# Expert loop of a hybrid decoder: one branch a step, chunk operations ahead of the next split, one transposition for crowded experts

## The chip, the cores and the metric

The kernel runs on one core of one Trainium2 chip, as one program. The metric is the device time of an execution in microseconds (us). Before the change three runs took 1495.41, 1495.72 and 1496.64 us; the median is 1495.72 us. The profiled execution took 1494.7 us, of which 1492.9 us lie between its first and last instruction (the span).

## What is computed

A trunk of two layers on 256 tokens of width 1024. Each layer has a mixer (a gated linear attention group and a state space group) and a feed-forward part. In the first layer that is a dense SwiGLU, in the second a mixture of eight SwiGLU experts, of which each token uses two:

```python
def moe_swiglu(h, router_w, w_gate, w_up, w_down):
    t = h.reshape(bsz * seq, d)
    logits = (t @ router_w).astype(jnp.float32)
    top_v, top_i = lax.top_k(logits, TOP_K)
    top_p = jax.nn.softmax(top_v, axis=-1)
    gates = jnp.sum(jax.nn.one_hot(top_i, N_EXPERTS) * top_p[..., None], axis=1)
    for e in range(N_EXPERTS):
        out = out + gates[:, e:e + 1] * swiglu(t, w_gate[e], w_up[e], w_down[e])
# swiglu(t, g, u, d) = (silu(t @ g) * (t @ u)) @ d;  g and u are 1024 x 3584, d is 3584 x 1024, all float32
```

A token without an expert has the gate zero there, so the kernel computes for each expert only the tokens that chose it.

## The kernel before

Every weight comes from memory as float32, in items of 1 MB (128 partitions by 2048 numbers), each once. It is split in two numbers of a reduced float32 type ("fp32r"): ScalarE writes the high part (L182), VectorE subtracts it from the original and writes the low part (L183). Products are then three matmuls: high by high, low by high, high by low. `pump` (L154) issues loads on SyncE's queue as soon as a raw buffer is free, that is, once its split is done. `fill` splits the next item into free slots; `w_done` frees the slots of an item whose matmuls have been issued, and calls `fill`. In the expert stage ten slots hold five split items, so what `w_done` issues after a step is the split of the item five steps later. The order in which operations are issued in the program is the order in which each engine's queue runs them.

The experts run one after the other, `run_experts` writing out the whole order. The hidden width 3584 is cut in seven chunks of 512. A chunk has six steps, one item each: gate (G) first and second half, up (U) first and second half, and down (D) first and second half of the chunk before. The very last chunk's down steps are called L. Up to 128 tokens of an expert are gathered into X, tokens on the matmul's stationary side, so that gate and up rows come out with tokens on partitions. After U's second half the chunk operations follow, each put at a step by `put` into `due`:

- `copy` (L1245): ScalarE copies the finished gate or up rows out of PSUM, at once
- `gate`: TensorE transposes the gate rows in four blocks (L1253 or L1255), ScalarE takes SiLU (L1273)
- `hidden`, two steps later: TensorE transposes the up rows, VectorE multiplies (L1283)
- `parted`, three steps later: ScalarE (L1293) and VectorE (L1294) split the product for the down steps

If an expert has at most 64 tokens ("narrow"), a token takes two rows, one for the high and one for the low part: two matmuls do instead of three (L1203, L1209), and instead of a transposition a matmul with the matrix `fold` adds the two rows (L1253). Else it is "wide": three matmuls (L1205, L1206, L1209) and plain transpositions (L1255). Which one holds is known only on the chip, so `modal` issues both forms in a branch (`tc.If`, L1193). The matmuls of a step have a branch on TensorE alone, each of `gate`, `hidden` and `parted` one on TensorE, ScalarE and VectorE. After a step's matmuls come, in this order: `done()` with the next split, then the chunk operations due, then `at`, which at given steps combines the expert before into the sum (L1624), and prepares the next one: its token maps, their transposition (`slots_T`, L1598), and its gathered and split tokens (`split_slots`, through `split_cols`, L498).

Experts are ordered on the chip so that full and sparse ones alternate; in this run places 1, 3 and 5 (from 0) are wide.

Of the kernel before, what the change touches and what calls it, by code (L numbers as in the profile page):

```python
# [17 lines left out]
P = 128  # L18
# [10 lines left out]
MOE_SLOTS = ("ra", "rb")  # L29
MOE_TURNED = 4  # L30
NH = 4
HALF = P // 2

HANDOFF_SPLITS = ((1, 1, 0, 1), (1, 1, 0, 1))
# [16 lines left out]
def trunk(ctx: ExitStack, tc: tile.TileContext, a: dict, out: bass.AP):  # L51
# [11 lines left out]
    def nm(s):  # L63
        uid[0] += 1
        return f"{s}_{uid[0]}"
# [4 lines left out]
    def ps_t():  # L70
        return psum.tile([P, 512], F, name=nm("pt"), tag="t", bufs=1)
# [261 lines left out]
    pe.transpose(pt[:, :DK], c_rows, ident[:DK, :DK])  # L333
    act.activation(s_col, pt[:, :DK], AF.Silu)

    tri = const.tile([P, P], F, name="tri")
    dve.tensor_scalar(tri, jp, 0.0, None, op0=OP.is_ge)
    btri = const.tile([P, P], F, name="btri")
    dve.tensor_scalar(btri, jp, 0.0, 1.0 / 16.0, op0=OP.is_ge, op1=OP.mult)
    dve.memset(btri[0:64, 64:128], 0.0)  # L340
    bmask = btri.bitcast(I32)
# [149 lines left out]
    def split_tmp(src, scale):  # L491
        return main.tile([P, len(scale), src.shape[-1]], F, name=nm("sct"), tag="rt", bufs=2)

    def split_cols(dst_h, dst_l, src, scale, shift=None):

        tmp = split_tmp(src, scale)
        scaled(act, tmp, src, scale, shift)
        dve.tensor_copy(dst_h, tmp)  # L498
        dve.tensor_tensor(dst_l, tmp, dst_h.bitcast(F), op=OP.subtract)

    def split_pair(a0, a1, mid=None):
# [733 lines left out]

    def run_experts(mo, experts, operand, fold, at):

        gs, us, sil, th, ys, ops = {}, {}, {}, {}, {}, {}
        due, ps = {}, {}
        order = list(moe_order(experts))  # L1240
        where = {t: n for n, t in enumerate(order)}

        def copied(tag, p):
            out = mo.tile([P, FC], F, name=nm(tag), tag=tag)
            act.activation(out, p, AF.Copy)  # L1245
            return out

        def folded(src, nar, p):

            for k in range(4):  # L1250
                ks = slice(k * P, (k + 1) * P)
                if nar:
                    pe.matmul(p[:, ks], src[:, ks], fold, start=True, stop=True)  # L1253
                else:
                    pe.transpose(p[:, ks], src[:, ks], ident)  # L1255
            return p

        def blocks(t, nar):
            return t.rearrange("p (k t) -> p k t", k=4)[:, :, :HALF if nar else P]

        def put(n, f, *args):
            due.setdefault(n, []).append((f, args))

        def copy(kind, key):
            (gs if kind == "G" else us)[key] = copied("gs" if kind == "G" else "us", ps.pop((kind,) + key))

        def gate(key):
            src, p = gs.pop(key), ps_t()
            s = sil[key] = mo.tile([P, FC], F, name=nm("fsg"), tag="fsg")

            def body(nar):
                folded(src, nar, p)
                act.activation(blocks(s, nar), blocks(p, nar), AF.Silu)  # L1273

            modal(ops[key[0]][2], body)

        def hidden(key):
            src, p, s = us.pop(key), ps_mm(), sil[key]

            def body(nar):  # L1280
                folded(src, nar, p)
                sv = blocks(s, nar)
                dve.tensor_tensor(sv, blocks(p, nar), sv, op=OP.mult)  # L1283

            modal(ops[key[0]][2], body)

        def parted(key):
            t = th[key] = mo.tile([P, 4, P, 2], R, name=nm("fth"), tag="fth", bufs=2)
            s = sil.pop(key)

            def body(nar):
                sv, tv = blocks(s, nar), t[:, :, :HALF if nar else P]
                act.activation(tv[:, :, :, 0], sv, AF.Copy)  # L1293
                dve.tensor_tensor(tv[:, :, :, 1], sv, tv[:, :, :, 0].bitcast(F), op=OP.subtract)  # L1294

            modal(ops[key[0]][2], body)

        for n, (kind, e, c, i) in enumerate(order):
            key = (e, c)
            if (kind, c, i) == ("G", 0, 0):  # L1300
                ops[e] = operand(e)
            X, narrow, _ = ops[e]
            if kind in "GU" and not i:
                ps[(kind,) + key] = ps_mm()
            if (kind, c, i) == ("D", 0, 0):
                ys[e] = ps_pair()
            parts, done = whole()
            dsts = []
            for k0, m, wh, wl in parts:
                for k in range(m):  # L1310
                    if kind in "GU":
                        kk = 4 * i + k0 + k
                        dsts.append((ps[(kind,) + key], X[:, kk], wh[:, k], wl[:, k], kk == 0, kk == 7))
                    elif kind == "L":
                        dsts.append((ys[e][i], th[key][:, k0 + k], wh[:, k], wl[:, k], False, k0 + k == 3))
                    else:
                        kk = 2 * i + k0 + k
                        for hf in range(2):
                            hs = slice(hf * 512, (hf + 1) * 512)
                            dsts.append((ys[e][hf], th[key][:, kk], wh[:, k, hs], wl[:, k, hs], c == 0 and kk == 0,  # L1320
                                         c == NFC - 1 and kk == 3))
            modal(narrow, lambda nar: mm_slots(dsts, nar))
            done()
            if kind in "GU" and i:
                put(n, copy, kind, key)
            if (kind, i) == ("U", 1):
                lag = 1 if key == (experts[-1], NFC - 1) else 2
                put(n, gate, key)
                put(n + lag, hidden, key)
                put(n + lag + 1, parted, key)  # L1330
            for f, args in due.pop(n, ()):
                f(*args)
            if kind in "GU":
                at(e, c, "GU".index(kind) * 2 + i, ys)
            elif kind == "D":
                e1, c1 = (e, c + 1) if c + 1 < NFC else (experts[experts.index(e) + 1], 0)
                at(e1, c1, 4 + i, ys)
            else:
                at(e, NFC, i, ys)
        assert not due  # L1340
        return ys[experts[-1]]
# [41 lines left out]
    def moe(mo, ys, row, mT):  # L1383
# [9 lines left out]
        mr = mo.tile([P, 2, 8], F, name="mr")  # L1393
        mb = mo.tile([P, 2, 8], BF, name="mb")
        gates = mo.tile([P, 2, 8], F, name="gates")
        pos = mo.tile([P, 2, 8], F, name="pos")
        cnt = mo.tile([P, 8], F, name="cnt")
        cmx = mo.tile([P, 1], F, name="cmx")
        cmi = mo.tile([P, 1], I32, name="cmi")
        shc = mods[:, l, 3]  # L1400
# [3 lines left out]
        pool.memset(onesb, 1.0)  # L1404
        iota_s = mo.tile([P, P], F, name="iota_s")
        pool.iota(iota_s, pattern=[[1, P]], base=0, channel_multiplier=0, allow_small_or_imprecise_dtypes=True)
        iota_h = mo.tile([P, P], F, name="iota_h")
        pool.iota(iota_h, pattern=[[1, HALF], [0, 2]], base=0, channel_multiplier=0, allow_small_or_imprecise_dtypes=True)
        fold = mo.tile([P, P], F, name="fold")
        pool.iota(fold, pattern=[[-2, P]], base=0, channel_multiplier=1, allow_small_or_imprecise_dtypes=True)  # L1410
        pm2 = mo.tile([P, 2, P], F, name="pm2")
        dve.tensor_scalar(pm2[:, 0], fold, 0.0, None, op0=OP.is_ge)
# [81 lines left out]
        pe.matmul(pp[:, 16:24], onesb, mb[:, 1], start=False, stop=True)  # L1494
        for t, r in enumerate((r0, r1)):
            dve.tensor_scalar(mr[:, t], mb[:, t], r, None, op0=OP.mult)
        dve.tensor_copy(pos, pp[:, 0:16].rearrange("p (t e) -> p t e", t=2))
        dve.tensor_scalar(few, pp[:, 16:24], float(HALF), None, op0=OP.is_le)

        def second_weights():  # L1500
# [2 lines left out]
            pool.tensor_tensor(pr[:, :, 1], euler, pr[:, :, 0], op=OP.pow)  # L1503

        def make_gates():
            dve.tensor_copy(cnt, pp[:, 16:24])
            dve.tensor_reduce(cmx, cnt, axis=AX.X, op=OP.max)
            dve.tensor_scalar(cmi, cmx, float(-P), 0.0, op0=OP.add, op1=OP.max)
            dve.tensor_scalar(pr[:, :, 0:1], pr[:, :, 1:2], 1.0, None, op0=OP.add)
            dve.reciprocal(pr[:, :, 0:1], pr[:, :, 0:1])  # L1510
            dve.tensor_tensor(pr[:, :, 1:2], pr[:, :, 1:2], pr[:, :, 0:1], op=OP.mult)
            for t in range(2):
                dve.tensor_scalar(gates[:, t], oh[:, t, 0], pr[:, t, 0:1], None, op0=OP.mult)
                dve.scalar_tensor_tensor(gates[:, t], oh[:, t, 1], pr[:, t, 1:2], gates[:, t], op0=OP.mult, op1=OP.add)
# [75 lines left out]
        def slots_T(e, pm, ps=ps_t, narrow=None):  # L1590
            pT = pTs[:, e % 2]
            p = ps()
            def body(nar):
                for t in range(2):
                    pe.transpose(p[:, t * P:(t + 1) * P], (pm2 if nar else pm)[:, t], ident)

            modal(narrow, body)
            dve.tensor_scalar(pT, p[:, :256].rearrange("p (t s) -> p t s", t=2), 0.0, None, op0=OP.is_gt)  # L1598
            return pT

        def y_split(y, hf, row=None):
# [73 lines left out]
        def split_slots(e, hf):  # L1675
            dst, (src, scale, shift) = gathered(e, hf), gather(m["pm"], hf, free)

            def body(nar):
                w = HALF if nar else P
                split_cols(*[d[:, :, :w] for d in dst], src[:, :, :w], scale, shift)  # L1680

            modal(narrow[e][1], body)

# [213 lines left out]
```

## Time and profile before

| | |
|---|---|
| median of three runs | 1495.72 us |
| profiled execution | 1494.7 us |
| its span | 1492.9 us |
| TensorE matmuls busy | 1400.3 us (94%) |
| VectorE busy | 1286.0 us (86%) |
| ScalarE busy | 1052.4 us (70%) |
| read from memory | 480.12 MB, 322 GB/s over the span |

Busy times of matmuls overlap, because the next starts before the one before has ended; where TensorE works without a gap the distance of starts tells its pace. The page cuts the span into 40 slices of 37.3 us; the experts take the time from about the sixteenth slice on. Idle time is listed with what ended it.

### The profile page before, as it was taken

To read this page: it belongs to the slowest core of one execution; us is meant where nothing else is said; L and a number is where in the kernel's file an instruction comes from. 1 tells how busy PE (TensorE), PEld (TensorE's weight loads), DVE (VectorE), ACT (ScalarE), POOL (GpSimd) and SP (SyncE) were. 2 spreads that over 40 slices of the span, in tenths; PEclk is the share of its full clock that TensorE was granted. 3 is DMA by queue.
4 is the path that set the end of the run, shared out by engine and by line. 5 is a ranking of instruction groups with operands and counts; after the bars stand their busy time and mean duration, and the time that the engine had idled before them with its cause. 6 is when DMAs were issued, how large, how long until landed. Compare 5 with 4: busy or idle time off the path is not lost.

```text
span 1492.9 us, 22114 instructions
## 1 busy us (share of the span) xinstructions
PE 1400.3 (94%) x7578; PEld 1200.1 (80%) x7578; DVE 1286.0 (86%) x1186; ACT 1052.4 (70%) x1255; POOL 46.6 (3%) x74
## 2 busy tenths in 40 slices
PE   5998899999999998999999999999999999998986
PEld 4886699999879776788888778888788888877764
DVE  7888877777766659999889999988999988999996
ACT  3484654544557557798778888778898777888885
POOL 2011000000010011000000000000000000000001
PEclk9999999999999998999999999999999999999998
DMA  9974678888844456999999999999999999999994
GB/s 345 313 253 164 231 277 311 314 312 320 298 170 142 150 174 221 342 394 393 393 341 370 393 393 395 393 364 366 390 394 392 394 375 357 387 393 395 393 392 153
DMA packets 204618, 483.29 MB, mean 324 GB/s; under 512 B 13119, under 2 KB 15405, under 8 KB 204462
## 3 DMA queue, kind: packets, MB, share of 16 engines
q1 hardware_dynamic: 203890, 480.05, 87.7%
q8 instruction: 99, 1.62, 0.5%
q10 hardware_dynamic: 428, 0.63, 0.1%
q0 software_dynamic: 144, 0.52, 0.1%
q14 instruction: 57, 0.47, 0.1%
HBM read 480.12 MB, written 1.05 MB: 322 GB/s over the span
## 4 chain that ended last, share of the span: by engine, by line
PE 69%; DVE 13%; DMA 6%; issue 6%; ACT 5%; POOL 1%; DVEq 0%; ACTq 0%; SPq 0%; POOLq 0%
PE mm L1209 9%; PE y L1209 5%; PE mm L1205 5%; PE mm L1206 5%; DVE ws L183 4%; PE mm L1203 4%; PE mm L430 4%; PE mm L429 4%; PE mm L431 4%; PE y L429 3%; PE y L431 3%; PE y L430 3%; PE y L1203 3%; PE y L1205 3%; PE y L1206 3%
## 5 line engine op out<-in xcount | busy, mean ns | idle before, releaser
L174 ACT ACTIVATE ws<-raw 128x1024 fp32r<-128x1024 f32 x136 | 143.9, 1061 | 139.6 <-PE mm L431 61.4
L183 DVE TENSOR_TENSOR ws<-raw,ws 128x2048 fp32r<-128x2048 f32 x97 | 222.1, 2291 | 15.9 <-ACT ws L182 15.8
L175 DVE TENSOR_TENSOR ws<-raw,ws 128x1024 fp32r<-128x1024 f32 x136 | 164.5, 1222 | 57.5 <-ACT ws L174 57.1
L182 ACT ACTIVATE ws<-raw 128x2048 fp32r<-128x2048 f32 x97 | 185.7, 1916 | 24.6 <-PE mm L1206 12.0
L1205 PE MATMUL mm<-ws,hTl 128*128 128x512 f32 x336 | 134.9, 402 | 0.0
L1206 PE MATMUL mm<-ws,hTl 128*128 128x512 f32 x336 | 132.6, 395 | 0.0
L1203 PE MATMUL mm<-ws,hTh 128*128 128x512 f32 x448 | 125.9, 403 | 4.9 <-ACT gs L1245 2.7
L1209 PE MATMUL y<-ws,fth 128*128 128x512 f32 x448 | 124.4, 400 | 0.0
L1209 PE MATMUL mm<-ws,hTh 128*128 128x512 f32 x448 | 122.4, 395 | 0.0
L1209 PE MATMUL mm<-ws,hTl 128*128 128x512 f32 x448 | 122.1, 394 | 0.0
L183 DVE TENSOR_TENSOR ws<-xm,ws 128x2048 fp32r<-128x2048 f32 x46 | 105.4, 2290 | 14.0 <-ACT ws L182 14.0
L367 DVE SCALAR_TENSOR_TENSOR ada<-raw,s_col,ada 128x1024 f32<-128x1024 f32 (+1 forms) x98 | 112.2, 1145 | 2.1
L183 DVE TENSOR_TENSOR ws<-xx,ws 128x2048 fp32r<-128x2048 f32 x47 | 107.7, 2291 | 7.2 <-ACT ws L182 7.0
L183 DVE TENSOR_TENSOR ws<-ada,ws 128x2048 fp32r<-128x2048 f32 x47 | 107.7, 2292 | 7.0 <-ACT ws L182 6.5
L183 DVE TENSOR_TENSOR ws<-xce,ws 128x2048 fp32r<-128x2048 f32 x47 | 107.7, 2292 | 5.9 <-ACT ws L182 5.8
L183 DVE TENSOR_TENSOR ws<-q,ws 128x2048 fp32r<-128x2048 f32 x47 | 107.6, 2290 | 4.2 <-ACT ws L182 3.7
L429 PE MATMUL mm<-hTh,ws 128*128 128x256 f32 x384 | 108.1, 281 | 0.0
L430 PE MATMUL mm<-hTh,ws 128*128 128x256 f32 x384 | 106.9, 278 | 0.0
L431 PE MATMUL mm<-hTl,ws 128*128 128x256 f32 x384 | 106.9, 278 | 0.0
L1209 PEld LDWEIGHTS y<-ws,fth 128*128 128x128 f32 x448 | 87.8, 196 | 19.3
L182 ACT ACTIVATE ws<-xm 128x2048 fp32r<-128x2048 f32 x46 | 88.1, 1916 | 18.7 <-PE mm L1206 8.3
L1209 PEld LDWEIGHTS mm<-ws,hTh 128*128 128x128 f32 x448 | 85.2, 190 | 19.4
(392 smaller groups left out, 3282.4 us busy)
## 6 DMA issues: line engine op xcount, KB each, us to landing
raw<-in_ada_w SPq DMA_DIRECT2D x48, 1024.0 KB, 5.8
raw<-in_moe_w_up SPq DMA_DIRECT2D x33, 1024.0 KB, 6.8
raw<-in_moe_w_gate SPq DMA_DIRECT2D x32, 1024.0 KB, 9.9
raw<-in_moe_w_down SPq DMA_DIRECT2D x32, 1024.0 KB, 12.5
raw<-in_w_in SPq DMA_DIRECT2D x21, 1024.0 KB, 5.3
ada<-in_moe_w_down SPq DMA_DIRECT2D x17, 1024.0 KB, 9.5
xx<-in_moe_w_gate SPq DMA_DIRECT2D x16, 1024.0 KB, 8.9
q<-in_moe_w_gate SPq DMA_DIRECT2D x16, 1024.0 KB, 12.8
```

The costliest lines, as they stand in the source:

```text
L174: act.activation(h, src, AF.Copy)
L175: dve.tensor_tensor(lo, src, h.bitcast(F), op=OP.subtract)
L182: act.activation(h, r, AF.Copy)
L183: low = lambda: dve.tensor_tensor(lo, r, h.bitcast(F), op=OP.subtract)
L367: dve.scalar_tensor_tensor(acc, w, s_col[:, k:k + 1], acc, op0=OP.mult, op1=OP.add)
L429: pe.matmul(ps, xh, wh, start=start, stop=False)
L430: pe.matmul(ps, xl, wh, start=False, stop=False)
L431: pe.matmul(ps, xh, wl, start=False, stop=stop)
L1203: pe.matmul(ps, xs[:, 0:HALF].rearrange("p s two -> p (s two)"), wh, start=start, stop=False)
L1205: pe.matmul(ps, xs[:, :, 0], wh, start=start, stop=False)
L1206: pe.matmul(ps, xs[:, :, 1], wh, start=False, stop=False)
L1209: pe.matmul(ps, both if nar else xs[:, :, 0], wl, start=False, stop=stop)
```

## The change

1. Inside `run_experts`, from chunk 3 of the first expert on (`LATE_SPLITS`), the chunk operations that fall on a step of the same expert go into the same branch as the step's matmuls, on three engines, and are issued before `done()`, so before the next split. Operations that fall on a step of another expert keep a branch of their own, and are issued before the split too.
2. Gate rows are taken out of PSUM at G's second half: as a copy in the narrow form, as SiLU in the wide one. In the wide form VectorE multiplies SiLU and up rows as they stand, and one transposition of the product follows at `parted`, three steps after U, from which ScalarE and VectorE split. In the narrow form the two folds stay, with SiLU after the first.
3. The first expert's first chunk has its `hidden` one step earlier.
4. `split_slots` has the cast of gathered tokens done by ScalarE; `slots_T` takes Sign on ScalarE where VectorE compared with zero.
5. `pos` and `cnt` come out of PSUM in one copy; `iota_h` and `fold` take the places of the causal masks `btri` and `tri`.

```diff
-    def split_cols(dst_h, dst_l, src, scale, shift=None):
+    def split_cols(dst_h, dst_l, src, scale, shift=None, eng=dve):
...
-        dve.tensor_copy(dst_h, tmp)
+        (dve.tensor_copy if eng is dve else lambda o, i: act.activation(o, i, AF.Copy))(dst_h, tmp)
...
+        def gate_rows(key):
+            p = ps.pop(("G",) + key)
+            g, w = gs[key], gw[key] = rows("gs"), rows("gw")
+            return lambda nar: act.activation(g if nar else w, p, AF.Copy if nar else AF.Silu)
+        def up_rows(key):
+            p, t = ps.pop(("U",) + key), rows("us")
+            us[key] = t
+            src, q = gs.pop(key), ps_t()
+            s = sil[key] = mo.tile([P, 4, HALF], F, name=nm("fsg"), tag="fsg")
             def body(nar):
+                act.activation(t, p, AF.Copy)
+                if nar:
+                    folded(src, nar, q)
+                    act.activation(s, blocks(q, nar), AF.Silu)
+            return body
...  hidden
+                if nar:
+                    folded(src, nar, p)
+                    dve.tensor_tensor(s, blocks(p, nar), s, op=OP.mult)
+                else:
+                    dve.tensor_tensor(w, w, src, op=OP.mult)
...  parted
+                if not nar:
+                    folded(w, nar, p)
+                sv, tv = s if nar else blocks(p, nar), t[:, :, :HALF if nar else P]
                 act.activation(tv[:, :, :, 0], sv, AF.Copy)
                 dve.tensor_tensor(tv[:, :, :, 1], sv, tv[:, :, :, 0].bitcast(F), op=OP.subtract)
...  the loop over steps
-            modal(narrow, lambda nar: mm_slots(dsts, nar))
-            done()
+            late = key >= LATE_SPLITS
             if kind in "GU" and i:
-                put(n, copy, kind, key)
+                put(n, gate_rows if kind == "G" else up_rows, key)
             if (kind, i) == ("U", 1):
-                lag = 1 if key == (experts[-1], NFC - 1) else 2
-                put(n, gate, key)
+                lag = 1 if key in ((experts[0], 0), (experts[-1], NFC - 1)) else 2
                 put(n + lag, hidden, key)
                 put(n + lag + 1, parted, key)
-            for f, args in due.pop(n, ()):
-                f(*args)
+            steps = due.pop(n, ())
+            here = [f(*args) for f, args in steps if late and args[0][0] == e]
+            if here:
+                def both(nar):
+                    mm_slots(dsts, nar)
+                    for f in here:
+                        f(nar)
+                modal(ops[e][2], both)
+            else:
+                modal(narrow, lambda nar: mm_slots(dsts, nar))
+                if not late:
+                    done()
+                for f, args in steps:
+                    modal(ops[args[0][0]][2], f(*args))
+            if late:
+                done()
...  slots_T
-            dve.tensor_scalar(pT, p[:, :256].rearrange("p (t s) -> p t s", t=2), 0.0, None, op0=OP.is_gt)
+            act.activation(pT, p[:, :256].rearrange("p (t s) -> p t s", t=2), AF.Sign)
```

## Rows read from the trace of the kernel before

**Rows 1.** The page: throughput in 40 slices of the span.
```profile
GB/s 345 313 253 164 231 277 311 314 312 320 298 170 142 150 174 221 342 394 393 393 341 370 393 393 395 393 364 366 390 394 392 394 375 357 387 393 395 393 392 153
```
**Rows 2.** Stretches of the expert stage: length, busy time of each engine, clock, DMA share, GB/s.
```profile
620.00:750.00 130.00, 128.43 (x629) 108.43 (x628) 123.96 (x84) 108.14 (x93) 0.00 (x0) 1.00 1.04 393
750.00:830.00 80.00, 80.00 (x386) 67.70 (x385) 69.95 (x45) 66.20 (x56) 0.00 (x0) 1.00 0.98 357
830.00:980.00 150.00, 145.59 (x708) 121.49 (x707) 143.95 (x99) 123.06 (x105) 0.00 (x0) 1.00 1.04 394
980.00:1060.00 80.00, 80.00 (x385) 67.66 (x384) 69.90 (x45) 66.10 (x57) 0.00 (x0) 1.00 1.00 366
1060.00:1210.00 150.00, 146.59 (x707) 122.94 (x706) 144.07 (x100) 123.73 (x104) 0.00 (x0) 0.99 1.04 393
1210.00:1300.00 90.00, 89.91 (x432) 75.59 (x431) 79.85 (x53) 72.99 (x64) 0.00 (x0) 1.00 1.00 369
1300.00:1460.00 160.00, 145.29 (x696) 119.38 (x695) 154.69 (x105) 132.76 (x114) 0.74 (x1) 0.96 1.04 393
```
**Rows 3.** The chain of waits in a wide expert: start, us, what.
```profile
1004.18 0.92 PE mm L1209 x4
1005.10 0.44 PE pt L1255 x4
```
**Rows 4.** Instructions at the end of a narrow expert: start, us, engine; idle before.
```profile
1121.22 2.29 DVE L183 TENSOR_TENSOR ws<-q,ws 128x2048 fp32r<-128x2048 f32 x1
...
1123.42 0.42 DVE L1283 TENSOR_TENSOR fsg<-mm,fsg 128x256 f32<-128x256 f32 x1
...
1123.75 2.28 DVE L183 TENSOR_TENSOR ws<-xce,ws 128x2048 fp32r<-128x2048 f32 x1
1123.93 0.44 ACT L1293 ACTIVATE fth<-fsg 128x256 fp32r<-128x256 f32 x1 [2.48 <-DVE fsg L1283]
1124.26 1.90 ACT L182 ACTIVATE ws<-raw 128x2048 fp32r<-128x2048 f32 x1
...
1126.06 0.58 ACT L1245 ACTIVATE gs<-mm 128x512 f32<-128x512 f32 x1
...
1126.70 1.16 PE L1253 MATMUL pt<-fold,gs 128*128 128x128 f32 x8 [1.21 <-ACT gs L1245]
```
**Rows 5.** Groups by line: count, busy us, mean ns, idle before.
```profile
L1255 PE MATMUL mm<-ident,us 128*128 128x128 f32 x84 | 12.6, 272 | 0.0
L1245 ACT ACTIVATE gs<-mm 128x512 f32<-128x512 f32 x56 | 32.4, 578 | 0.0
L1283 DVE TENSOR_TENSOR fsg<-mm,fsg 128x512 f32<-128x512 f32 x21 | 14.4, 684 | 0.0
```
**Rows 6.** The chain of waits in the same narrow expert.
```profile
1119.94 0.15 issue
```
**Rows 7.** Groups by line on VectorE: combination, splits, casts, token maps.
```profile
L1624 DVE SCALAR_TENSOR_TENSOR acc<-y,order,acc 128x512 f32<-128x512 f32 x24 | 16.9, 750 | 0.0
L1608 DVE TENSOR_TENSOR yl<-y,yh 128x512 fp32r<-128x512 f32 x14 | 9.6, 686 | 0.0
L498 DVE CAST hTl<-sct 128x512 fp32r<-128x512 f32 x6 | 2.6, 432 | 0.0
L1598 DVE TENSOR_SCALAR pTs<-y 128x256 fp32r<-128x256 f32 x8 | 3.4, 419 | 0.0
```
**Rows 8.** Instructions: the masks' last matmuls, and GpSimd's writing of a constant.
```profile
491.42 1.95 PE L877 MATMUL y<-tri,la 128*128 128x128 f32 x16
...
530.12 0.82 POOL L1408 IOTA iota_h<- 128x128 f32 x1
```
**Rows 9.** Instructions behind the last weight's landing.
```profile
1469.71 1.92 ACT L182 ACTIVATE ws<-ada 128x2048 fp32r<-128x2048 f32 x1 [0.19 <-DMA ada<-in_moe_w_down]
1471.66 2.29 DVE L183 TENSOR_TENSOR ws<-ada,ws 128x2048 fp32r<-128x2048 f32 x1 [0.30 <-ACT ws L182]
```
**Rows 10.** Groups by line: ScalarE's table loads with the last SiLU of a mixer.
```profile
L1077 ACT ACT_TABLE_LOAD x2 | 2.6, 1283 | 0.0
```

More of the change, by code (lines that the diff above doesn't have):

```diff
@@ L31 @@
 NH = 4
+LATE_SPLITS = (0, 3)
 HALF = P // 2
@@ L334, in trunk @@
     act.activation(s_col, pt[:, :DK], AF.Silu)
-    tri = const.tile([P, P], F, name="tri")
+    tri = const.tile([P, P], F, name="tri", tag="tri")
     dve.tensor_scalar(tri, jp, 0.0, None, op0=OP.is_ge)
-    btri = const.tile([P, P], F, name="btri")
+    btri = const.tile([P, P], F, name="btri", tag="btri")
     dve.tensor_scalar(btri, jp, 0.0, 1.0 / 16.0, op0=OP.is_ge, op1=OP.mult)
@@ L1236, in run_experts @@
     def run_experts(mo, experts, operand, fold, at):
-        gs, us, sil, th, ys, ops = {}, {}, {}, {}, {}, {}
+        gs, gw, us, sil, hid, th, ys, ops = {}, {}, {}, {}, {}, {}, {}, {}
         due, ps = {}, {}
@@ L1241, in run_experts, with rows @@
         where = {t: n for n, t in enumerate(order)}
[L1243 to L1246, printed above, removed]
+        def rows(tag):
+            return mo.tile([P, FC], F, name=nm(tag), tag=tag)
         def folded(src, nar, p):
@@ L1262, in put @@
             due.setdefault(n, []).append((f, args))
[L1264 to L1269, printed above, removed]
-            def body(nar):
-                folded(src, nar, p)
-                act.activation(blocks(s, nar), blocks(p, nar), AF.Silu)
-            modal(ops[key[0]][2], body)
+        def gate_rows(key):
+            p = ps.pop(("G",) + key)
+            g, w = gs[key], gw[key] = rows("gs"), rows("gw")
+            return lambda nar: act.activation(g if nar else w, p, AF.Copy if nar else AF.Silu)
@@ L1277, in hidden @@
+        def up_rows(key):
[3 more added lines that the diff above has]
+            s = sil[key] = mo.tile([P, 4, HALF], F, name=nm("fsg"), tag="fsg")
+            def body(nar):
+                act.activation(t, p, AF.Copy)
[3 more added lines that the diff above has]
+            return body
         def hidden(key):
-            src, p, s = us.pop(key), ps_mm(), sil[key]
+            src, s, w = us.pop(key), sil[key], gw[key]
+            p = hid[key] = ps_mm()
@@ L1280, in body @@
             def body(nar):
[L1281 to L1285, printed above, removed]
+                if nar:
[3 more added lines that the diff above has]
+                    dve.tensor_tensor(w, w, src, op=OP.mult)
+            return body
         def parted(key):
             t = th[key] = mo.tile([P, 4, P, 2], R, name=nm("fth"), tag="fth", bufs=2)
-            s = sil.pop(key)
+            s, p, w = sil.pop(key), hid.pop(key), gw.pop(key)
@@ L1291, in body @@
             def body(nar):
-                sv, tv = blocks(s, nar), t[:, :, :HALF if nar else P]
+                if not nar:
+                    folded(w, nar, p)
+                sv, tv = s if nar else blocks(p, nar), t[:, :, :HALF if nar else P]
                 act.activation(tv[:, :, :, 0], sv, AF.Copy)
                 dve.tensor_tensor(tv[:, :, :, 1], sv, tv[:, :, :, 0].bitcast(F), op=OP.subtract)
-            modal(ops[key[0]][2], body)
+            return body
         for n, (kind, e, c, i) in enumerate(order):
@@ L1395, in moe @@
         gates = mo.tile([P, 2, 8], F, name="gates")
-        pos = mo.tile([P, 2, 8], F, name="pos")
-        cnt = mo.tile([P, 8], F, name="cnt")
+        poscnt = mo.tile([P, 24], F, name="poscnt")
+        pos, cnt = poscnt[:, 0:16].rearrange("p (t e) -> p t e", t=2), poscnt[:, 16:24]
         cmx = mo.tile([P, 1], F, name="cmx")
@@ L1406, in moe @@
         pool.iota(iota_s, pattern=[[1, P]], base=0, channel_multiplier=0, allow_small_or_imprecise_dtypes=True)
-        iota_h = mo.tile([P, P], F, name="iota_h")
+        iota_h = const.tile([P, P], F, name="iota_h", tag="btri")
         pool.iota(iota_h, pattern=[[1, HALF], [0, 2]], base=0, channel_multiplier=0, allow_small_or_imprecise_dtypes=True)
-        fold = mo.tile([P, P], F, name="fold")
+        fold = const.tile([P, P], F, name="fold", tag="tri")
         pool.iota(fold, pattern=[[-2, P]], base=0, channel_multiplier=1, allow_small_or_imprecise_dtypes=True)
@@ L1496, in moe @@
             dve.tensor_scalar(mr[:, t], mb[:, t], r, None, op0=OP.mult)
-        dve.tensor_copy(pos, pp[:, 0:16].rearrange("p (t e) -> p t e", t=2))
+        dve.tensor_copy(poscnt, pp[:, 0:24])
         dve.tensor_scalar(few, pp[:, 16:24], float(HALF), None, op0=OP.is_le)
@@ L1505, in make_gates @@
         def make_gates():
-            dve.tensor_copy(cnt, pp[:, 16:24])
             dve.tensor_reduce(cmx, cnt, axis=AX.X, op=OP.max)
@@ L1679, in body @@
                 w = HALF if nar else P
-                split_cols(*[d[:, :, :w] for d in dst], src[:, :, :w], scale, shift)
+                split_cols(*[d[:, :, :w] for d in dst], src[:, :, :w], scale, shift, act)
             modal(narrow[e][1], body)
```

## The prediction

> **What bounds the kernel now.** I read the page's throughput by slices first [rows 1], over a span of 1492.9 us: from the eighteenth slice on mostly 390 to 395 GB/s. That is the expert stage, about 575 to 1470 us, in which 336 items of 1.0486 MB arrive. Every change of weight lies in it, so I cut it into stretches [rows 2]. In four of seven the DMA moves 393 to 394 GB/s at a busy share of 1.04: it is full, and one item takes 1.0486/0.3935 = 2.66 us. In the other three, 80, 80 and 90 us long, it falls to 357, 366 and 369. What is lost there is 80 x (1 - 357/393.5) = 7.4 us, 80 x (1 - 366/393.5) = 5.6 us and 90 x (1 - 369/393.5) = 5.6 us, 18.6 us together. In the first two of these TensorE is busy all the time and VectorE 70 of 80 us, so TensorE holds the transfers back.
>
> The chain of waits in a dip says why [rows 3]: nothing but TensorE. These are experts with over 64 tokens ("wide", at places 1, 3 and 5; "narrow" are the others). Four matmuls take 0.92 us, a step has twelve (2.78 us), a chunk of six steps 16.7 us and two groups of four transpositions at 0.44 us: 17.6 us against 6 x 2.66 = 16.0 us of transfer. Each wide expert thus falls behind by 7 x 1.6 = 11 us plus its gathers; the buffers take up most, and what they can't take is the dip.
>
> The second loss is TensorE's own idle time in the narrow expert before: 130 - 128.4, 150 - 145.6 and 150 - 146.6, so 1.6, 4.4 and 3.4 us [rows 2]. One instance was followed [rows 4]: ScalarE waits 2.48 us for the product of VectorE, which stands behind three splits of VectorE; then it splits another weight, copies the gate rows at 1126.06, and only then can TensorE transpose them, after 1.21 us of idling, though weights for three more steps lay ready.
>
> **The change part by part.** *One transposition in wide chunks.* SiLU and product run on rows, and one result is turned in place of gate and up. Per chunk one group of four goes, 0.44 us [rows 3]; the 84 instructions that turn up rows are 3 experts x 7 chunks x 4, and as many turn gate rows [rows 5]. So 7 x 0.44 = 3.1 us per wide expert, 9.2 us in all, on the path, since TensorE has no gap there. ScalarE loses one copy of 0.58 us per chunk [rows 5]; VectorE does the same two operations of 0.68 us and about as much with one operand moved between PSUM and SBUF, which I cost at nothing (bounds -0.1 and +0.1 us each, off the path where VectorE is 70 of 80 us busy).
>
> *Chunk operations ahead of the next split.* Five split weights fit ahead of the matmuls, so the split issued after step n is that of item n+5, and the gate copy of step n stands behind it on ScalarE; TensorE needs that copy two steps later and can come no nearer than three items to the split edge. After the change the copy stands behind the split of item n+4, and TensorE can come within two. It enters a wide expert one item nearer, which is one supply interval: 2.20 us by VectorE's pace (1121.22 to 1123.42 [rows 4]) to 2.66 us by the transfers, so 2.4 us; no more than the idle time it has, 1.6 us before the first wide expert. Sum: 1.6 + 2.4 + 2.4 = 6.4 us. What is queued behind the operations that now wait earlier: the split of item n+5 and, behind it on VectorE, its low part, then SP's next load, which needs that buffer. In the narrow form ScalarE's SiLU now waits for TensorE's fold (about 0.81 us: its eight matmuls) ahead of that split, and VectorE's product for the second fold. While TensorE is less than four items behind, both folds are done when the queue gets there; where it is five behind, VectorE waits for it anyway. I take 2 us over the stage for small waits; ends 0 and the price of rival D.
>
> *One branch a step.* Per chunk TensorE has 6 branches in place of 9, ScalarE and VectorE 4 in place of 3. Beside VectorE's product the trace shows a sequencer piece of 0.15 us [rows 6], yet the 0.42 us product is followed by the next operation 0.33 us after its start [rows 4]: the branch is hidden under the queue. Taken as 0; upper end 0.15 x 53 late chunks = 8 us if that cover is gone, lower end -2 us for the branches TensorE loses.
>
> *VectorE to ScalarE.* Fourteen casts of the gathered tokens (0.43 us wide) and eight token maps (0.42 us) leave VectorE [rows 7], some 1.2 us per expert. ScalarE, 133 of 160 us busy at the end [rows 2], has room. I count it as what pays for the smaller waits, no gain of its own; from 0 to -4 us.
>
> *The rest.* The two constants that take over the places of the causal masks are written by GpSimd at 530 us; the masks' last readers, TensorE's matmuls with `tri`, end by 493.4 us [rows 8], so nothing waits. One copy of 24 columns for two saves 0.16 us in the first expert. Nothing.
>
> *The end.* The last weight is split at 1469.71 behind the step before the last up step; the up copy, the folds and the last matmul follow it both ways, and VectorE's last split still stands ahead of the product [rows 9]. The 23 us behind that landing stay.
>
> Sum for the dips: the first loses 3.1 + 1.6 = 4.7 of 7.4 us, the others 5.5 each of 5.6: 15.7, less 2: 13.7 us. Nothing after the last dip (1300 us) can gain, because there the DMA is full. The profiled execution took 1494.7 us with what lies around the span, 1.0 us under the median of 1495.72; applied to the median: 1482.0.
>
> **The Trainium skill against the trace.** The token maps become a Sign on ScalarE, a function that the kernel doesn't use now. The trace has nine table loads of 1283 ns, the last two with a SiLU of the mixer [rows 10], none in the expert loop, where SiLU, Copy and Identity alternate. If Sign needs other tables, each of eight maps brings two loads, 2.57 us: that is rival C. "ScalarE: Activation LUTs" in the Trainium skill, section "Table sets: the hidden batching unit", says that functions come in sets, that cheap ones (relu, copy, identity, abs; Sign is not in that list) are in every set, and that a switch costs one load. The trace agrees for Copy and Identity; for Sign no run so far shows it. By the worst reading of the rule the time is C's, by the other the forecast's.
>
> **The rivals.**
> A, the forecast: 1482.0, own range 1477 to 1488. For it: gapless TensorE in the dips and a full DMA elsewhere.
> B, the dips are half VectorE's: in the last ten or twenty microseconds of each the next narrow expert has begun, with its combining (four operations of 0.75 us [rows 7]) on a full VectorE. If that part, about 1.4 us each (4.2), stays and the nearer approach brings nothing, 9.2 - 4.2 = 5 us remain: 1490.7. Against it: a backlog is one quantity, and less of it at the end of a wide expert is also less for VectorE.
> C, Sign reloads tables: 8 x 2 x 1.283 = 20.5 us of ScalarE; hidden where it has slack, paid in the four or so experts where VectorE is full: about 8 us, 13.7 - 8 = 5.7: 1490.0.
> D, slower: in narrow chunks the operations ahead of the split hold up VectorE. VectorE needs 6 x 2.20 + 2 x 0.33 = 13.9 us per chunk of 16.0, plus per expert four combinations of 0.75, two splits of 0.69, two casts of 0.43 and a map of 0.42 [rows 7], 5.7 us or 0.8 per chunk: 1.3 us of slack. It decides when the new waits exceed 1.3 us a chunk. If both folds and the SiLU are waited for in full, 0.81 + 0.38 + 0.81 = 2.0 us, 0.7 x 35 narrow chunks = 24.5 us are lost, less 9.2: 1511. Against it: ScalarE ran ahead of VectorE in the narrow expert [rows 4], so a hold of one microsecond is covered.
> E, all goes well: all 18.6 us, and some of the start of the stage, where 575 to 610 us are below full throughput too: 1474.
> F, TensorE's saving is swallowed by VectorE's limit at once: no change, 1495.
>
> **How the numbers follow.** A 0.50, B 0.17, C 0.07, D 0.14, E 0.06, F 0.06. The time is A's. The range 1474 to 1498 holds A, B, C, E and F and leaves D out, with its bounds of branches (8 us) inside. A measurement can't tell a change under 0.2% (3 us) from none: faster 0.50 + 0.06 + most of B and C (0.20) = 0.76; same 0.06 + 0.04 = 0.10; slower 0.14.
>
> **What would show it.** Right: in wide chunks one group of four transpositions a chunk (84 in all) and a period of 17.1 us; throughput in the three dips at 380 GB/s or more; ScalarE's gate copy ahead of the split, TensorE's idle time before it gone in the narrow experts that precede a wide one; no table load in the expert loop; the end unchanged behind the last landing. Wrong: new idle time of VectorE on ScalarE's splits in narrow experts, throughput under 390 there, or dips as deep as before although the transpositions are gone.

## The result: slower by 0.6%, and the profile after

The changed kernel takes 1505.29 us (median of nine runs, 1500.7 to 1508.85) against 1496.52 for the one before on the same chip: ratio 1.006, interval 1.0048 to 1.0072. It was forecast at 1482.0 with a range to 1498. The profiled execution took 1508.06 us, span 1506.2.

The page's throughput, to be read against [rows 1]: the three dips (341 and 370, 364 and 366, 375 and 357 before) are deeper, each by about as much; their lowest slices are 322, 344 and 340 in place of 341, 364 and 357.

```profile
GB/s 346 307 251 169 225 290 311 317 311 318 297 147 157 143 168 224 352 371 392 382 322 375 393 392 395 391 344 365 394 394 391 389 361 340 388 393 396 392 393 148
```

One window, 670 to 1300 us, holds the three dips in either kernel: length, busy time of PE, PEld, DVE, ACT and POOL, clock, DMA share, GB/s. First before, then after:

```profile
670.00:1300.00 630.00, 622.09 (x2984) 522.80 (x2983) 581.98 (x385) 515.41 (x432) 0.00 (x0) 1.00 1.02 382
```
```profile
670.00:1300.00 630.00, 611.59 (x2868) 509.12 (x2868) 571.99 (x365) 505.18 (x425) 0.00 (x0) 0.99 1.01 377
```

Against the full 393.5 GB/s of the prediction, 630 x (1 - 382/393.5) = 18.4 us are lost there before, and 26.4 after: 8.0 us more, nearly all of the 8.8 between the medians. TensorE works 10.5 us less in the window and the transfers move less: it waits more. That dips stay deep although 84 transpositions are gone is one of the signs of being wrong that the prediction had named. "Dip loss" below is this figure, good to 0.8 us since GB/s are whole numbers.

To see where, I cut at the experts' borders (a wide stretch runs from the first to the last matmul of a wide expert's form). Before: the first wide stretch (the other two are 139.68 as well) and the narrow one after it.

```profile
671.27:810.96 139.69, 139.69 (x656) 117.89 (x654) 123.89 (x80) 110.45 (x91) 0.00 (x0) 1.00 1.01 373
810.96:901.76 90.80, 86.39 (x441) 71.64 (x440) 90.50 (x64) 78.84 (x71) 0.00 (x0) 1.00 1.04 392
```

After: the three wide stretches, then the narrow one behind the first.

```profile
676.46:816.19 139.73, 137.55 (x627) 114.70 (x626) 124.11 (x78) 108.10 (x88) 0.00 (x0) 1.00 1.00 365
905.66:1049.28 143.62, 139.04 (x627) 115.87 (x626) 124.72 (x78) 109.45 (x88) 0.00 (x0) 0.99 1.01 373
1138.41:1283.79 145.38, 140.11 (x627) 116.64 (x626) 124.75 (x78) 109.25 (x88) 0.00 (x0) 0.98 1.00 370
816.19:905.66 89.47, 86.62 (x441) 71.62 (x440) 88.01 (x60) 78.45 (x73) 0.00 (x0) 1.00 1.04 393
```

Before, TensorE never paused in a wide stretch (busy 139.69 of 139.69). After, it idles 2.2, 4.6 and 5.3 us, and its busy time rises from 137.55 to 140.11 though its work is the same. The narrow stretch became 1.3 us shorter (the second, from 90.78 to 89.13, 1.65); TensorE's wait for the gate copy there fell from 3.9 and 3.3 us to 1.4 in each.

The first expert, which is narrow, went the other way. From its first matmul to that of the first wide expert, before and after:

```profile
567.04:671.27 104.23, 96.41 (x469) 79.83 (x469) 103.36 (x94) 88.37 (x76) 4.88 (x1) 0.95 0.90 336
```
```profile
569.93:676.46 106.53, 97.38 (x468) 79.30 (x469) 100.35 (x88) 87.70 (x79) 2.69 (x1) 0.95 0.89 330
```

It is 2.3 us longer. ScalarE waits there 16.2 us for VectorE's product (L1303) where it waited 7.4, the splits that now stand behind wait with it, and VectorE, which had waited 0.2 us for ScalarE's splits, waits 4.4:

```profile
DVE ws L184 <- ACT ws L183: 4.4, 6, 1.4
```

So of the 13.3 us between the two profiled spans 9.7 lie in the wide stretches and 2.3 in the first expert, the two narrow stretches give back 3.0, 2.9 lie ahead of the experts (where the first expert starts anywhere from 563.2 to 569.9 us in the kernels tried here) and 1.4 behind the third wide stretch.

The waits of TensorE in the third wide stretch (total, times, longest) name what holds it there:

```profile
PE mm L1254 <- DVE gw L1292: 4.0, 2, 3.6
PE mm L1206 <- ACT ws L183: 0.8, 1, 0.8
PE mm L1206 <- PEq L1194: 0.5, 1, 0.5
```

L1292 is VectorE's product in the row form, L1254 the transposition of it. The instructions at the longest of these waits (start, length, engine, what; idle before):

```profile
1156.79 1.91 ACT L183 ACTIVATE ws<-raw 128x2048 fp32r<-128x2048 f32 x1 [1.43 <-DMA raw<-in_moe_w_up]
...
1158.74 2.29 DVE L184 TENSOR_TENSOR ws<-raw,ws 128x2048 fp32r<-128x2048 f32 x1 [1.05 <-ACT ws L183]
...
1160.95 0.68 DVE L1292 TENSOR_TENSOR gw<-gw,us 128x512 f32<-128x512 f32 x1
...
1161.78 1.08 PE L1254 MATMUL mm<-ident,gw 128*128 128x128 f32 x4 [3.60 <-DVE gw L1292]
...
1163.52 0.63 PE L1206 MATMUL mm<-ws,hTl 128*128 128x512 f32 x1
1163.94 0.63 PE L1207 MATMUL mm<-ws,hTl 128*128 128x512 f32 x1
...
1167.65 0.39 PE L1206 MATMUL mm<-ws,hTl 128*128 128x512 f32 x1
1167.88 0.40 PE L1207 MATMUL mm<-ws,hTl 128*128 128x512 f32 x1
```

Read it backwards. The transposition waits for the product; the product has no wait of its own, it stands behind a low-part split; that one waits for ScalarE's high part, and that for the load. A wide expert is entered close behind the transfers, so TensorE, for one transposition, has to wait for a weight that it needs only later. The same product was 0.54 and 2.92 us late in the first and second wide expert. Of the 12.0 us that TensorE idles in the three stretches, 8.2 are waits for this product, 2.3 for its own sequencer (PEq, explained under e1 and e3) and 1.6 for weights. Afterwards matmuls start 0.42 us apart (1163.94 - 1163.52) in place of 0.23, until 1167.65. The window around it:

```profile
1160.00:1170.00 10.00, 8.22 (x27) 6.77 (x28) 7.93 (x7) 6.83 (x7) 0.00 (x0) 0.66 1.05 389
```

The granted clock averages 0.66 over these ten microseconds, between the levels of 1.2 and 2.4 GHz; the slower matmuls are the rise in busy time.

### The profile page after: what moved, and what is told of

Same layout as the page of the kernel before. It is cut to its first block, busy times and chain, and to the rows that moved or that the text cites. A ratio compares the mean times of both kernels' runs of the same rounds, so it can differ in the third digit from the quotient of the medians.

```text
span 1506.2 us, 22031 instructions
## 1 busy us (share of the span) xinstructions
PE 1403.7 (93%) x7494; PEld 1196.6 (79%) x7494; DVE 1279.1 (85%) x1163; ACT 1046.1 (69%) x1256; POOL 44.4 (3%) x74
## 5 line engine op out<-in xcount | busy, mean ns | idle before, releaser
L1206 PE MATMUL mm<-ws,hTl 128*128 128x512 f32 x336 | 137.8, 410 | 3.8 <-PEq L1194 2.2
L1207 PE MATMUL mm<-ws,hTl 128*128 128x512 f32 x336 | 134.2, 399 | 0.0
L1210 PE MATMUL mm<-ws,hTl 128*128 128x512 f32 x448 | 122.9, 396 | 0.8 <-DVE ws L184 0.8
L184 DVE TENSOR_TENSOR ws<-xx,ws 128x2048 fp32r<-128x2048 f32 x47 | 107.4, 2286 | 10.5 <-ACT ws L183 10.3
L1210 PEld LDWEIGHTS mm<-ws,hTl 128*128 128x128 f32 x448 | 86.9, 194 | 19.1 <-DVE ws L184 1.5
```

The lines of the kernel that those rows point to most:

```text
L184: low = lambda: dve.tensor_tensor(lo, r, h.bitcast(F), op=OP.subtract)
L1206: pe.matmul(ps, xs[:, :, 0], wh, start=start, stop=False)
L1207: pe.matmul(ps, xs[:, :, 1], wh, start=False, stop=False)
L1210: pe.matmul(ps, both if nar else xs[:, :, 0], wl, start=False, stop=stop)
```

## The experiments

Three theories stood at the start. W: the product, now one step ahead of its transposition and behind a split, holds TensorE where a wide expert begins. O: the chunk operations ahead of the split and the merged branches cost everywhere. M: the cast and the Sign on ScalarE cost. From the first traces came D: a branch with a side that is empty on an engine makes that engine run dry. Ratios are to the kernel before on the same chip, with 95% intervals; single executions scatter by some us. All kernels compute the whole result.

**e2: two turns again, all else changed.** The diff is the row form taken back (gate and up turned apart, SiLU and product in turned form).

> The changed kernel, but wide chunks turn gate and up rows apart as before; branches and order as changed. Theory W: wide stretches near 139.7 us each and nothing gained from the transposition: 1493 to 1498 us. Theory O: the cost stays and the saved transposition is lost as well: 1505 to 1512. Theory M: 1505 to 1510.

1495.36 us, ratio 0.9987 (0.9973 to 1.0), dip loss 16.8. The new order and the merged branches cost nothing on the whole, they bring about 2 us. O falls as the cause of the loss, and most of it lies in the row form or its place in this order. Not all: the first expert takes 106.3 us here too, 2.1 more than before, against the two other narrow stretches' 89.1 and 89.0 us in place of 90.8.

**e4: cast and Sign back on VectorE** (`eng=dve`, `OP.is_gt` for `AF.Sign`).

> The changed kernel with the cast of gathered tokens and the token map back on VectorE. Theory M: 1494 to 1499 us. Theories W and O: 1503 to 1508, no change from the changed kernel within its scatter.

1504.97, ratio 1.0051 (1.0031 to 1.0071). M falls; the moves bring nothing either.

**e1: the product two steps earlier**, three ahead of its transposition.

```
 def up_rows(key):                       # body
-    act.activation(t, p, AF.Copy)
     if nar:
+        act.activation(t, p, AF.Copy)
         ...
+    else:
+        dve.tensor_tensor(w, w, p, op=OP.mult)   # and none in hidden()
```

> The changed kernel, but in wide chunks VectorE multiplies SiLU by the up rows straight out of PSUM at the second up step, three steps before the product is transposed, in place of one step. Theory W: the loss comes from the product standing one step before its transposition and behind a split, so that TensorE stands idle and slows down on entering a wide expert (143.6 and 145.4 us there for 139.7 before). Then the wide stretches come to about 137 us each and the time to 1486 to 1493 us, below the kernel before. Theory O (the operations ahead of the splits, or the merged branches, cost time everywhere): 1502 to 1507. Theory M (cast and Sign on ScalarE): 1502 to 1507.

1502.48, ratio 1.0036 (1.0021 to 1.005): W missed by over nine. The wide stretches did come down (139.3, 139.5 and 139.3 us) and the product is waited for no more, but each narrow stretch takes 92.1 us in place of 89.5 and 89.1, the first expert 109.4 in place of 106.5, and there are new waits:

```profile
DVE ws L184 <- DVEq L1194: 9.0, 23, 0.5
PE mm L1254 <- DVEq L1194: 2.6, 3, 1.1
```

L1194 is the branch; q marks an engine's sequencer. The product in `up_rows` leaves VectorE's narrow side empty there, and `hidden`'s wide side too. Two things had been changed at once; from this came D.

**e3: the row form in the old order, with separate branches** (`LATE_SPLITS = (NE, 0)`).

> The changed kernel with the old order throughout: the next split ahead of the chunk operations, branches apart; one transposition stays. Theory W: the product now stands behind one more split, TensorE is held longer on entering a wide expert: 1506 to 1514 us. Theory O: 1488 to 1494, since the cause is gone and the saving stays. Theory M: 1503 to 1508.

1539.22, ratio 1.0284 (1.0261 to 1.0307), dip loss 60: all three theories missed, O by 45 us. TensorE's waits, 560 to 1500 us:

```profile
PE mm L1204 <- PEq L1194: 16.0, 28, 0.9
PE mm L1254 <- DVE gw L1292: 14.8, 18, 1.7
```

In the program an empty side holds, in place of work, a wait for the engine's own last instruction: on TensorE 170 such waits stand in this kernel, 25 in the changed one, 2 in the one before. The trace has 77 of them on the sides that were taken; 72 left TensorE idle, 0.3 to 0.9 us each, 36.9 us together.

**e9: the same with the empty sides filled.** `pe.matmul(junk[:, 0:8], ident, ident[:, 0:8])` on each side that is empty on TensorE; no more such waits are left in the program than before the change.

> The kernel with the row form in the old order and with a branch of their own for all chunk operations (1539 us, ratio 1.028 to before), with a small matmul of eight columns added on every branch side that is empty on TensorE. Nothing is left out. Its own trace had 73 waits of TensorE for its sequencer, 35.7 us together. Theory D (an empty side makes the engine run dry): these waits go, and in wide chunks, where two of them lie in each, the period falls from 19.4 to 17.3 us: 1500 to 1510 us. If the sequencer waits are the branches themselves, whatever they hold: 1530 us or more, the waits still there.

1526.29, ratio 1.0215 (1.0199 to 1.0231). No wait for the sequencer is left, so the waits are the empty sides'. But D's time is missed: 13 of 43 us came back by the medians, 10 by the ratios, since other waits grew, the product's again. TensorE's waits, 560 to 1500 us:

```profile
PE mm L1254 <- DVE gw L1292: 24.7, 18, 2.7
PE pt L1252 <- ACT gs L1268: 23.6, 15, 4.1
```

In the old order the product stands one split further back, so it is late in nearly every wide chunk (18 times). The filling costs as well:

```profile
737.31 1.09 PE L1210 MATMUL mm<-ws,hTl 128*128 128x512 f32 x4
738.24 0.28 PE L1356 MATMUL pt<-ident 128*128 128x8 f32 x2
738.38 0.48 PE L1206 MATMUL y<-ws,fth 128*128 128x512 f32 x1
738.69 0.39 PE L1207 MATMUL y<-ws,fth 128*128 128x512 f32 x1
```

0.14 us until the next matmul, and that one's successor 0.31 behind it in place of 0.23: 0.22 us a time, two in a wide chunk, as much as the transposition saved.

**e5: the changed kernel with the empty sides filled** (they lie in the steps between two experts and in the first expert's first three chunks, which keep the old order).

> The changed kernel with one more small matmul of eight columns on those branch sides that are empty on TensorE in the steps run between two experts (the product's wide side, the split's narrow side); nothing else changes and nothing is left out. Theory D (an empty side makes the engine run dry before it goes on): the changed kernel's trace has seven such waits of TensorE, 4.2 us together, two of them (1.3 us) in the first wide expert; they go, so 1499 to 1503 us, and the holds of the transposition for VectorE's product (0.5, 2.9 and 3.6 us) stay. Theory W (only those holds cost): the TensorE waits may go, but the time stays at 1503 to 1507. Either way the first wide stretch tells: 139.7 us now, 138.5 by D.

1500.79, ratio 1.0041 (1.0026 to 1.0056): 2.8 us better than the changed kernel by the ratios, whose intervals overlap, 4.5 by the medians: the time that D said. The three wide stretches sum to 426.0 us in place of 428.7. The first, which was to decide, came out between the two, at 139.2 us (139.7 by W, 138.5 by D). Where the sequencer waits went, the product's wait grew: at the three entries it was 0.54, 2.92 and 3.60 us, here 1.34, 4.45 and 3.61. The second of them:

```profile
923.99 0.66 PE L1254 MATMUL mm<-ident,gw 128*128 128x128 f32 x4 [4.45 <-DVE gw L1292]
```

**e6: the transposition two steps behind the product.** The buffer edit keeps the gate rows' place free.

```
+gw[key] = src                           # in hidden()
...
-put(n + lag + 1, parted, key)
+put(n + lag + (1 if c == NFC - 1 else 2), parted, key)
...
-dve.tensor_tensor(w, w, src, op=OP.mult)
+dve.tensor_tensor(src, w, src, op=OP.mult)      # parted turns src
```

> The changed kernel with the transposition and the split of the hidden rows two steps behind the product in place of one, in all chunks but an expert's last; the product is written over the up rows, so that the gate rows' buffer comes free as before. Empty branch sides stay. Theory W (the product, one step ahead of its transposition and behind a weight's split on VectorE, holds TensorE as a wide expert begins, and the granted clock falls after it): the holds of 0.5, 2.9 and 3.6 us and the slower matmuls after them go, 1494 to 1499 us, second and third wide stretch at 139.7 like the first. Theory D (empty sides alone): 1502 to 1507. If narrow chunks pay for the later split, which their down steps need, narrow stretches grow over 89.5 us each.

1489.92 us, ratio 0.9963 (0.995 to 0.9976): 15 us under the changed kernel, and faster than both. W came true, and the time is 4 us below its range. The wide stretches:

```profile
667.87:806.79 138.92, 137.28 (x628) 114.87 (x626) 122.88 (x77) 105.56 (x86) 0.00 (x0) 1.00 1.00 370
896.30:1036.46 140.16, 137.52 (x627) 114.77 (x626) 123.92 (x78) 109.22 (x88) 0.00 (x0) 1.00 1.02 384
1125.28:1264.22 138.94, 137.40 (x628) 114.73 (x626) 123.88 (x78) 109.29 (x88) 0.00 (x0) 1.00 1.03 383
```

They sum to 418.0 us against 428.7, 10.7 us less; busy time is equal in all three, the clock 1.00. The dip loss is 15.2. The same place in the third expert: the product still stands behind a split, but the transposition has come one step behind it.

```profile
1144.59 2.29 DVE L184 TENSOR_TENSOR ws<-raw,ws 128x2048 fp32r<-128x2048 f32 x1 [0.35 <-ACT ws L183]
...
1146.80 0.69 DVE L1293 TENSOR_TENSOR us<-gw,us 128x512 f32<-128x512 f32 x1
...
1147.63 0.63 PE L1254 MATMUL mm<-ident,us 128*128 128x128 f32 x4
```

The edit moves the narrow chunks' split a step later too. The two narrow stretches between wide ones did not pay for it (89.5 and 88.8 us), and the first expert won by it:

```profile
564.42:667.87 103.45, 93.03 (x468) 76.58 (x469) 100.91 (x89) 90.93 (x81) 2.68 (x1) 1.00 0.90 336
```

3.1 us less than in the changed kernel. ScalarE's wait for the narrow product falls there from 16.2 to 4.4 us. The stretch is 103.5 us in e7 as well, which has the same edit, and 106.1 to 106.5 in the changed kernel, e2, e4, e5 and e8, which don't. So e6 mends two things: the hold in the wide stretches, 10.7 us, and ScalarE's hold in the first expert, 3.1.

**e7: both, e6 with the sides filled.**

> The two edits before together: the transposition two steps behind the product, and the empty sides filled on TensorE. If W and D are all that went wrong, the one transposition's saving is left: TensorE works 137.4 us per wide stretch in the changed kernel against 139.7 before, so stretches of 137.5 us and 1487 to 1494 us, under the kernel with two turns (1495). If TensorE's work in the wide stretch doesn't set the end (theory N), stretches shorten, the narrow ones grow by as much, and the time stays with that of two turns, 1493 to 1498.

1489.78, ratio 0.9967 (0.9954 to 0.998), dip loss 15.2: the same as e6. The first wide stretch is 137.5 us, as forecast, the second 142.0, the third 139.8: the product is late again, by 1.9 and 2.0 us in the second and third wide expert, and in the second the granted clock fell after it (0.99 over the stretch). What the filling gives TensorE at the entry it waits for a moment later.

**e8: the row form in chunks 1 to 5 alone**; chunks 0 and 6 turned twice (`inside(key)` is `0 < c < NFC - 1`).

> The changed kernel with the row form in a wide expert's chunks 1 to 5 alone; the first and the last chunk are turned twice as before, so that the step between two experts has no side that is empty on TensorE and no product is waited for at the start of a wide expert. By W and D: no hold, no drain, five transpositions of 0.44 us saved per wide expert, 2.2 us each, 6.6 in all below the kernel with two turns: 1488 to 1492 us. By N (TensorE's work in the wide stretch doesn't set the end): 1493 to 1498. If the hold merely moves to the next chunk, as the wait of a product behind a split does in any chunk that is entered close behind the weights: 1498 to 1505, with a wait of TensorE for the product some 17 us later.

1499.12, ratio 1.0027 (1.0012 to 1.0041). The third case came in: the hold moved to the next chunk, here in the second wide expert.

```profile
939.43 0.63 PE L1254 MATMUL mm<-ident,gw 128*128 128x128 f32 x4 [3.90 <-DVE gw L1303]
```

The other two are 0.47 and 3.92 us. So it is not the border between experts: wherever the first transposition one step behind its product falls close behind the transfers, it waits.

**e10: e9 with the transposition two steps behind the product.**

> The same with the transposition and the split two steps behind the product: the one transposition alone, in the order and with the branches of before. If the one transposition's saving (0.44 us a chunk, twenty-one chunks, 9.2 us by the prediction) reaches the end when no hold and no empty side is in its way: 1487 to 1492 us, about what the new order with the same mending takes (1490). If it needs the new order: 1493 to 1500. If the old order, in which the transposition comes one place later behind the splits, holds TensorE all the same: over 1500, with waits for VectorE's product in wide chunks.

1506.99, ratio 1.008 (1.0067 to 1.0092). By its time the third case came in. The holds left most wide chunks (3 in place of 18), but the run can't answer its question: its wide chunk takes 787.60 - 770.02 = 17.58 us, as long as before, because two fillings of 0.22 us eat the transposition's 0.43. What one transposition is worth in the old order stays open.

Over all twelve kernels the median less the dip loss lies between 1474.6 and 1479.3 us, while the medians lie 49 us apart. So most of the difference between them arises in this one window.

## Why the prediction was wrong

**The step that failed** is the first of the change: "So 7 x 0.44 = 3.1 us per wide expert, 9.2 us in all, on the path, since TensorE has no gap there", with VectorE's operations costed "at nothing". The size was right. A clean wide chunk after takes 788.37 - 771.20 = 17.17 us, before 798.08 - 780.48 = 17.60. Before (the transposition of the up rows):

```profile
780.48 0.60 PE L1255 MATMUL mm<-ident,us 128*128 128x128 f32 x4
...
798.08 0.60 PE L1255 MATMUL mm<-ident,us 128*128 128x128 f32 x4
```

After (that of the product):

```profile
771.20 0.60 PE L1254 MATMUL mm<-ident,gw 128*128 128x128 f32 x4
...
788.37 0.60 PE L1254 MATMUL mm<-ident,gw 128*128 128x128 f32 x4
```

What failed was the "no gap". I priced the product by its duration and not by its place: before, TensorE needed a wide product only through its split, for the down steps; after, TensorE needs it one step later, with a weight's split, and so the transfer, in between. The saving of 6.8 us of busy time in the three stretches became 9.7 us of loss: 12.0 us idle, 8.2 of them for the product, and 4.5 us more busy time than e6 has, at the lower clock (1.5 and 2.7 in the second and third stretch). e6 put one step more between product and transposition, and 10.7 us went from the wide stretches.

**Even mended, the term is smaller.** e6 stands 3.6 us below e2, which keeps two turns, by the ratios (0.0024 x 1496; the intervals touch), 5.4 by the medians, not 9.2, and by their profiles more of that is the first expert (103.5 us against 106.3), where nothing is transposed, than the wide stretches (418.0 against 419.7). There TensorE saves 6.8 us of busy time in e6 too, but idles 1.6, 2.6 and 1.5 us: 2.3 for its sequencer, 2.2 for the product, 1.5 for weights. My reading, which no run isolates: at its start a wide expert is as fast as its weights arrive, and what is saved there turns into waiting.

**The chunk operations ahead of the split**: right in kind, about half in size. 6.4 less 2 us were counted; order and branches together gave about 2 us (e2, interval 0 to 4), and the second and third narrow stretch became 1.3 and 1.65 us shorter, not 2.4. The first, counted at 1.6 us of gain, became 2.3 us longer: there ScalarE stands at the product's split (16.2 us in place of 7.4) with the weights' splits now behind it. The prediction had taken "2 us over the stage for small waits"; this one stretch lies 3.9 us off. That the later split of e6 and e7 brings it to 103.5 us is what points to ScalarE's hold.

**One branch a step, "taken as 0"**: right for merged branches, wrong for those left alone. The row form empties sides on TensorE in the steps between experts and in the first expert's first chunks: seven waits, 4.2 us in the changed kernel, of which filling returned 3 to 4.5 (e5, at the edge of the noise), and nothing once the hold was mended (e7). The bound of 8 us held, the mechanism wasn't seen.

**The moves to ScalarE** brought nothing (e4), as one end of the range said. Rival C falls: both kernels have nine table loads, the last at 518 us, so none is loaded in the expert loop, where the eight Signs stand between SiLU and Copy. Of the two readings of "ScalarE: Activation LUTs" in the Trainium skill, section "Table sets: the hidden batching unit", the cheap one holds here.

```profile
L1618 ACT ACTIVATE pTs<-y 128x256 fp32r<-128x256 f32 x8 | 3.1, 384 | 0.0
```

**Rival D**, the one on the slower side, named the right engine, and for most of the loss the wrong place: it looked for VectorE's delay in narrow chunks. Its sign, new idle time of VectorE on ScalarE's splits, came mainly in the first expert (0.2 us before, 4.4 after), at 2.3 us; the next two narrow stretches (0.2 before, 1.3 after in each) came out shorter. F let VectorE swallow the saving, but that TensorE would lose by waiting for VectorE in a wide chunk stood in none of the rivals.

**The end**: the order changed, the length hardly. The last fold now waits for the SiLU that stands behind ScalarE's last split and the copy of the up rows.

```profile
1482.31 1.91 ACT L183 ACTIVATE ws<-ada 128x2048 fp32r<-128x2048 f32 x1 [0.69 <-DMA ada<-in_moe_w_down]
1484.13 0.58 ACT L1277 ACTIVATE us<-mm 128x512 f32<-128x512 f32 x1
...
1484.61 0.38 ACT L1280 ACTIVATE fsg<-pt 128x256 f32<-128x256 f32 x1
...
1485.03 2.08 PE L1252 MATMUL mm<-fold,us 128*128 128x128 f32 x8 [2.46 <-ACT fsg L1280]
```

From the last high part to the end of the span are 1506.2 - 1482.31 = 23.9 us, 0.7 more than before (1492.9 - 1469.71 = 23.2, [rows 9]). That is no more than single executions differ: with the same end it is 22.4 us in e2 and e6 and 23.8 in e4.

## What to carry to other kernels

When work moves from one engine to another, write down for each result who needs it next, how many steps later, and what stands ahead of its producer in that engine's queue; a gapless engine stays gapless only if that distance survives. A producer that stands behind a step waiting for a transfer needs its consumer at least two steps away here: three changed lines that moved the transposition and the split a step later turned 0.6% slower into 0.4% faster. Look at each stage apart, too: the first expert lost most of what the next narrow ones won, and no total showed it. And a test that moves an operation between branch sides may empty a side: count such sides before trusting its time.

## What the hardware showed

A branch whose taken side holds nothing for TensorE left it idle for 0.3 to 0.9 us in 72 of 77 cases (e3), since the program has a wait for the engine's own last instruction there; with a small matmul on these sides no such wait is left (e9). On VectorE it cost up to 0.5 us ahead of a split (e1).

After holds of 2.9 to 4.45 us for the product (two each in the changed kernel, e4, e5 and e8) TensorE's matmuls started 0.42 to 0.43 us apart in place of 0.23, in the case shown for some 4 us (1163.5 to 1167.65, granted clock 0.66 over 1160 to 1170). After holds of 0.5 to 1.7 us, as at the first wide entry of the changed kernel and of e3, the clock of the next ten microseconds was 1.00. In between it went both ways: a hold of 1.9 us in e7 was followed by slow matmuls, and one of 2.7 us in e9 was not.
